# Seven-product feed-forward: each product of a set in its own PSUM tile, six tiles in rotation; the last spill begun from GpSimd's queue

## The chip, the core and the metric

The kernel runs on one core of a Trainium2 chip. The time is the device time of one execution of the whole program in microseconds, the median of several runs. TensorE multiplies matrices into PSUM, VectorE and ScalarE read PSUM and SBUF, GpSimd works on SBUF alone, and SyncE (SP) begins most of the DMAs. Each engine executes its own instructions strictly in their order and waits on semaphores for the others.

## The reference

A decoder trunk of two layers on 1024 tokens of width 1024, in float32. Each layer is a mixer (a pooling and state-space mixer in layer 0, two kinds of attention in layer 1) and a feed-forward, each followed by a layer norm. The change lies in the feed-forward, which is the same code for both layers:

```python
def swiglu(x, w_gate, w_up, w_down):
    return (jax.nn.silu(x @ w_gate) * (x @ w_up)) @ w_down

# in each layer
x = layer_norm(DEEPNORM_ALPHA * x + swiglu(x, w_gate[l], w_up[l], w_down[l]), g[l], b[l])
```

with `w_gate` and `w_up` of 1024 x 2816 and `w_down` of 2816 x 1024.

## The kernel before

**Seven products.** `ffn` computes each matrix product as a 2 x 2 block product with seven products of half-size blocks instead of eight (the Winograd form of Strassen's scheme): sums of blocks are formed first, seven products follow, and further sums put the result together. Each float32 operand is kept as a high part and a low part (`operand`: ScalarE's cast writes the high part, L195, VectorE's subtraction the low part, L203), and one product of operands takes three matmuls, high by high, high by low, low by high (L496 to L498).

**First half.** 2816 features are 22 tiles of 128, taken in 11 pairs. For each pair there is an even set (gate) and an odd set (up): 22 sets of seven products each. A product is 4 blocks of k by 3 matmuls of 128 x 128 by 128 x 512, 12 matmuls in one PSUM bank. `load` brings the weights of a set, `prep` forms the block sums and the operands for the set ahead, `prod` issues the matmuls, and `step(s, i)` does product i of set s with the additions on VectorE that use it. From the fourth set on the order is 1, 6, 2, 7, 5, 4, 3. Line by line: L509 is ScalarE's copy of product 1 into `u`, L519 adds product 6, L523 product 2, L527 product 7, L530 and L531 product 5, L535 product 4, L538 product 3. ScalarE applies SiLU to the gate's results (L545); GpSimd multiplies them by the up results (L543). `spill` forms four sums on GpSimd (L555 to L558) and stores seven blocks to DRAM (`parts`) from SP's queue (L562). `residual` scales the residual rows on GpSimd (L620, L621) and stores them from GpSimd's queue.

**PSUM.** There are eight banks: four tiles of one bank, `p0` to `p3`, and the tile `pa` of two banks, which exists twice. Products 1 and 2 of a set share one single tile one after the other, product 6 has another, products 7 and 5 are the two halves of one `pa`, and products 4 and 3 the two halves of the other `pa`. A wait is kept for each tile: product 5 into the second half waits until VectorE has read product 7 out of the first half.

**Second half.** `second` multiplies by `w_down` in the same way: the blocks come back from `parts` (`load2`, into `hr`), `prep2` forms the operands, and for each of seven products 11 steps of 12 matmuls (L628 to L630) go into four banks, one after three matmuls; the first product uses p0 to p3. `prep2` of the first product also replaces a quarter of each weight tile by a difference (L614), at once.

**What sets the order.** The program is written in one order; a scheduler then places the instructions on each engine's queue by their dependences and free buffers. SBUF holds 50 slots of 128 x 1024 that all tiles of these stages share, so a load waits until a slot is free.

Of the kernel before, what the change touches and what calls it, by code (L numbers as in the profile page):

```python
# [15 lines left out]
ALU = mybir.AluOpType  # L16
# [3 lines left out]
P = 128  # L20
# [60 lines left out]
class Trunk:  # L81
# [364 lines left out]
    def ffn(self, l, ln, store, rows, parts, nxt=None):  # L446
# [6 lines left out]
        nc, ap = self.nc, self.ap  # L453
        lo, hi = slice(0, 512), slice(512, 1024)
        mm = nc.tensor.matmul
        tt = nc.vector.tensor_tensor
        pt = nc.gpsimd.tensor_tensor
        n_pairs = NFF // 2
# [31 lines left out]
        def prod(s, i, out, ks=range(4)):  # L490
            a, b = ops[s][i], x7[i]
            if ks[-1] == 3:
                del ops[s][i]
            for k in ks:
                ah, al = a[:, k * P:(k + 1) * P], a[:, 512 + k * P:512 + (k + 1) * P]
                mm(out=out, lhsT=ah, rhs=b[k][:, lo], start=k == 0, stop=False)  # L496
                mm(out=out, lhsT=ah, rhs=b[k][:, hi], start=False, stop=False)  # L497
                mm(out=out, lhsT=al, rhs=b[k][:, lo], start=False, stop=k == 3)  # L498

        hid = {}  # L500

        def step(s, i, ks=range(4)):

            up = s % 2
            if i == 1:
                x = self.ps("p2" if up else "p0", 1)
                open_[s] = {"x": x, "u": self.slot(name="u")}
                prod(s, 1, x)
                nc.scalar.copy(out=open_[s]["u"][:, lo], in_=x)  # L509
                return  # L510
            o = open_[s]
            u, x = o["u"], o["x"]
            if i == 6:
                if ks[0] == 0:
                    o["v"] = self.ps("p3" if up else "p1", 1)
                v = o["v"]
                prod(s, 6, v, ks)
                if ks[-1] == 3:
                    tt(out=u[:, hi], in0=u[:, lo], in1=v, op=ALU.add)  # L519
            elif i == 2:  # L520
                prod(s, 2, x)
                o["c"] = [self.slot(name="c" if up else "h") for _ in range(2)]
                tt(out=o["c"][0][:, lo], in0=u[:, lo], in1=x, op=ALU.add)  # L523
            elif i == 7:
                o["wz"] = self.pa()
                prod(s, 7, o["wz"][:, lo])
                tt(out=u[:, lo], in0=u[:, hi], in1=o["wz"][:, lo], op=ALU.add)  # L527
            elif i == 5:
                prod(s, 5, o["wz"][:, hi])
                tt(out=o["c"][1][:, hi], in0=u[:, lo], in1=o["wz"][:, hi], op=ALU.add)  # L530
                tt(out=u[:, hi], in0=u[:, hi], in1=o["wz"][:, hi], op=ALU.add)  # L531
            elif i == 4:
                o["wz"] = self.pa()
                prod(s, 4, o["wz"][:, lo])
                tt(out=o["c"][1][:, lo], in0=u[:, lo], in1=o["wz"][:, lo], op=ALU.add)  # L535
            else:
                prod(s, 3, o["wz"][:, hi])
                tt(out=o["c"][0][:, hi], in0=u[:, hi], in1=o["wz"][:, hi], op=ALU.add)  # L538
            if i in (4, 3):
                c = o["c"][i == 4]  # L540
                if up:
                    h = hid[s // 2][i == 4]
                    pt(out=h, in0=h, in1=c, op=ALU.mult)  # L543
                else:
                    nc.scalar.activation(out=c, in_=c, func=AF.Silu)  # L545
                    hid.setdefault(s // 2, [None, None])[i == 4] = c
            if i == 3:
                del open_[s]

        def spill(p):  # L550

            h0, h1 = hid.pop(p)
            a11, a12, a21, a22 = h0[:, lo], h1[:, lo], h0[:, hi], h1[:, hi]
            s12, s34 = self.slot(name="s"), self.slot(name="s")
            pt(out=s12[:, lo], in0=a21, in1=a22, op=ALU.add)  # L555
            pt(out=s12[:, hi], in0=s12[:, lo], in1=a11, op=ALU.subtract)
            pt(out=s34[:, lo], in0=a11, in1=a21, op=ALU.subtract)
            pt(out=s34[:, hi], in0=a12, in1=s12[:, hi], op=ALU.subtract)  # L558
            for i, src in ((1, a11), (2, a12), (4, a22), (5, s12[:, lo]), (6, s12[:, hi]), (7, s34[:, lo]),
                           (3, s34[:, hi])):  # L560
                at = ((i - 1) * n_pairs + p) * P
                nc.sync.dma_start(out=parts[at:at + P, :], in_=src)  # L562


        flat = [(i, p) for i in (1, 6, 5, 2, 3, 7, 4) for p in range(n_pairs)]
        hr, we, wo, ops2 = {}, {}, {}, {}
        loaded = [self.load_ahead - 1]

        def load2(n):
            if n >= len(flat):  # L570
                return
            i, p = flat[n]
            if p % 2 == 0:
                m = min(2, n_pairs - p)
                at = ((i - 1) * n_pairs + p) * P
                r = self.slot(name="hr")
                nc.sync.dma_start(out=r[:, 0:m * 512].rearrange("p (a c) -> p a c", c=512),
                                  in_=parts[at:at + m * P, :].rearrange("(a p) c -> p a c", p=P))
                hr[i, p] = r[:, lo]
                if m > 1:  # L580
                    hr[i, p + 1] = r[:, hi]
            for w, first, k in ((we, 1, 0), (wo, 6, 1)):
                if i == first:
                    w[p] = self.load_raw(ap["ffn_w_down"][l, (2 * p + k) * P:(2 * p + k + 1) * P, :])

        def prep2(n):
            if n >= len(flat):
                return
            i, p = flat[n]
            a = self.operand(hr.pop((i, p)), None, "h")  # L590
            e, o = we[p], wo.get(p)
            last = []
            if i == 1:
                b = e[:, lo]
                last.append((e[:, lo], e[:, hi], e[:, lo], ALU.subtract))
            elif i == 6:
                b = self.slot(name="t")[:, lo]
                tt(out=b, in0=o[:, hi], in1=e[:, lo], op=ALU.subtract)
            elif i == 5:
                b = e[:, lo]  # L600
            elif i == 2:
                b = o[:, lo]
            elif i == 3:
                b = o[:, hi]
                last.append((o[:, lo], o[:, lo], o[:, hi], ALU.subtract))
            elif i == 7:
                b = e[:, hi]
                tt(out=b, in0=o[:, hi], in1=b, op=ALU.subtract)
            else:
                b = o[:, lo]  # L610
                tt(out=b, in0=b, in1=e[:, lo], op=ALU.add)
            ops2[n] = a, self.operand(b, None, "w")
            for out, in0, in1, op in last:
                tt(out=out, in0=in0, in1=in1, op=op)  # L614

        accs = []
# [74 lines left out]
        def leads():  # L691
            for i in (1, 2):
                for s in range(2):
                    step(s, i)
                if i == 1:
                    yield
            load(2)
            for g in (1, 2, 2):
                next(preps[g])
            yield  # L700
            step(2, 1)
            for k in range(4):
                for s in range(2):
                    step(s, 6, range(k, k + 1))
                if k == 0:
                    yield
                    step(2, 2)
                if k < 3:
                    yield
# [6 lines left out]
        for s in range(n_sets):  # L716
# [22 lines left out]
            if s == n_sets - 2:  # L739
                for n in range(self.load_ahead):  # L740
                    load2(n)
        vs = [self.slot(name="v") for _ in range(2)]
        spill(n_pairs - 1)
        x7 = self.x7 = None
        main = second()
# [1136 lines left out]
```

## Time and profile before

| | |
|---|---|
| median of three runs | 2664.48 us (2663.90 to 2668.51) |
| profiled execution, its own time | 2659.8 us |
| span of its instructions | 2657.9 us |
| TensorE busy | 94% of the span |
| VectorE, ScalarE, GpSimd busy | 69%, 39%, 28% |
| mean granted TensorE clock | 0.983 |

Busy time is the share of the span in which an engine has an instruction under way. The time outside the span, 1.9 us, belongs to no engine. The two feed-forwards' first halves run from about 520 to 996 us and from about 1955 to 2429 us of the span; their second halves follow at once.

### The profile page before, as it was taken

To read this page: it belongs to the slowest core of one execution; us is meant where nothing else is said; L and a number is where in the kernel's file an instruction comes from. 1 tells how busy PE (TensorE), PEld (TensorE's weight loads), DVE (VectorE), ACT (ScalarE), POOL (GpSimd) and SP (SyncE) were. 2 spreads that over 40 slices of the span, in tenths; PEclk is the share of its full clock that TensorE was granted. 3 is DMA by queue.
4 is the path that set the end of the run, shared out by engine and by line. 5 is a ranking of instruction groups with operands and counts; after the bars stand their busy time and mean duration, and the time that the engine had idled before them with its cause. 6 is when DMAs were issued, how large, how long until landed. Compare 5 with 4: busy or idle time off the path is not lost.

```text
span 2657.9 us, 31492 instructions
## 1 busy us (share of the span) xinstructions
PE 2509.7 (94%) x11886; PEld 2012.1 (76%) x11886; DVE 1832.9 (69%) x2922; ACT 1038.4 (39%) x1742; POOL 731.1 (28%) x408
## 2 busy tenths in 40 slices
PE   8999999999899899999999999999989989898998
PEld 6788777777777777887787777777767777777887
DVE  4454555787676758976655566787787676766988
ACT  3333434442222233463344455664452222222443
POOL 2544531114342521212011122111014252433103
PEclk9999999999999999999999999999999999999999
DMA  4111114223333337322100011112323333324742
GB/s 164 48 32 40 40 41 154 80 91 116 110 123 107 127 119 295 125 95 90 66 25 32 24 40 38 34 60 69 111 79 132 103 133 104 131 81 184 266 147 75
DMA packets 93847, 261.46 MB, mean 98 GB/s; under 512 B 9696, under 2 KB 9952, under 8 KB 93696
## 3 DMA queue, kind: packets, MB, share of 16 engines
q1 hardware_dynamic: 86496, 234.23, 25.6%
q0 software_dynamic: 4448, 15.27, 1.7%
q10 hardware_dynamic: 2752, 9.96, 1.0%
q8 instruction: 93, 1.52, 0.2%
q14 instruction: 58, 0.48, 0.1%
HBM read 185.89 MB, written 71.30 MB: 97 GB/s over the span
## 4 chain that ended last, share of the span: by engine, by line
PE 75%; DVE 13%; issue 5%; ACT 3%; POOL 2%; DMA 1%; SPq 0%; DVEq 0%; ACTq 0%; POOLq 0%
PE pa L496 5%; PE pa L498 5%; PE pa L497 5%; PE pa L236 5%; PE pa L238 4%; PE pa L237 4%; PE pa L1589 4%; DVE w L203 4%; PE p L236 3%; PE p L238 3%; PE p L237 3%; PE p L498 3%; PE p L496 3%; PE p L497 3%; PE p L1659 3%
## 5 line engine op out<-in xcount | busy, mean ns | idle before, releaser
L203 DVE TENSOR_TENSOR w<-wr,w 128x512 fp32r<-128x512 f32 x440 | 387.4, 897 | 80.4 <-ACT w L195 79.8
L195 ACT CAST w<-wr 128x512 fp32r<-128x512 f32 x440 | 252.8, 619 | 454.9 <-DVE wr L479 279.5
L496 PE MATMUL pa<-x,w 128*128 128x512 f32 x704 | 283.7, 406 | 64.1 <-DVE u L527 63.8
L543 POOL TENSOR_TENSOR h<-h,c 128x1024 f32<-128x1024 f32 x44 | 113.9, 2588 | 651.7 <-issue 449.3
L497 PE MATMUL pa<-x,w 128*128 128x512 f32 x704 | 282.5, 401 | 0.0
L498 PE MATMUL pa<-x,w 128*128 128x512 f32 x704 | 282.1, 401 | 0.0
L203 POOL TENSOR_TENSOR wl<-wr,wh 128x1024 fp32r<-128x1024 f32 (+2 forms) x55 | 130.6, 2377 | 447.9 <-ACT wh L195 414.6
L496 PEld LDWEIGHTS pa<-x,w 128*128 128x128 f32 x704 | 136.1, 193 | 109.6 <-DVE u L527 77.2
L496 PE MATMUL p<-x,w 128*128 128x512 f32 x528 | 207.3, 394 | 6.9 <-ACT w L195 6.9
L498 PE MATMUL p<-x,w 128*128 128x512 f32 x528 | 206.9, 392 | 0.1
L497 PE MATMUL p<-x,w 128*128 128x512 f32 x528 | 206.7, 392 | 0.1
L498 PEld LDWEIGHTS pa<-x,w 128*128 128x128 f32 x704 | 136.5, 194 | 30.2
L497 PEld LDWEIGHTS pa<-x,w 128*128 128x128 f32 x704 | 137.2, 195 | 27.9 <-DVE x L203 0.7
L236 PE MATMUL pa<-xh,wh 128*128 128x512 f32 x368 | 149.1, 405 | 1.9 <-ACT u L895 1.1
L238 PE MATMUL pa<-xh,wl 128*128 128x512 f32 x368 | 144.5, 393 | 4.3 <-POOL wl L203 4.3
L629 PE MATMUL p<-w,h 128*128 128x512 f32 x352 | 139.3, 396 | 7.2 <-DVE w L203 7.1
L237 PE MATMUL pa<-xl,wh 128*128 128x512 f32 x368 | 144.2, 392 | 0.0
L628 PE MATMUL p<-w,h 128*128 128x512 f32 x352 | 138.1, 393 | 5.8 <-ACT w L195 5.8
L630 PE MATMUL p<-w,h 128*128 128x512 f32 x352 | 138.2, 392 | 0.0
L203 DVE TENSOR_TENSOR h<-hr,h 128x512 fp32r<-128x512 f32 x154 | 124.2, 807 | 16.9 <-ACT h L195 16.8
L195 ACT CAST h<-hr 128x512 fp32r<-128x512 f32 x154 | 95.2, 618 | 91.2 <-DMA hr<-parts 65.7
L496 PEld LDWEIGHTS p<-x,w 128*128 128x128 f32 x528 | 99.7, 189 | 28.7 <-ACT w L195 8.0
(391 smaller groups left out, 6084.2 us busy)
## 6 DMA issues: line engine op xcount, KB each, us to landing
hr<-parts SPq DMA_DIRECT2D x70, 512.0 KB, 4.6
wr<-in_ffn_w_gate_dram SPq DMA_DIRECT2D x44, 512.0 KB, 4.2
wr<-in_ffn_w_up_dram SPq DMA_DIRECT2D x44, 512.0 KB, 4.3
parts<-s SPq DMA_DIRECT2D x88, 256.0 KB, 2.1
wr<-in_ffn_w_down_dram SPq DMA_DIRECT2D x44, 512.0 KB, 9.7
parts<-h SPq DMA_DIRECT2D x66, 256.0 KB, 2.1
accr<-rows SPq DMA_DIRECT2D x32, 512.0 KB, 3.6
wr<-in_even_wt_dram SPq DMA_DIRECT2D x24, 512.0 KB, 3.6
```

Source lines behind the costliest of these rows:

```text
L195: self.nc.scalar.copy(out=out, in_=in_)
L203: eng.tensor_tensor(out=out, in0=in_, in1=hi.bitcast(F32), op=ALU.subtract)
L236: mm(out=out, lhsT=lh, rhs=rh, start=i == 0, stop=False)
L237: mm(out=out, lhsT=lh, rhs=rl, start=False, stop=False)
L238: mm(out=out, lhsT=ll, rhs=rh, start=False, stop=i == n - 1)
L496: mm(out=out, lhsT=ah, rhs=b[k][:, lo], start=k == 0, stop=False)
L497: mm(out=out, lhsT=ah, rhs=b[k][:, hi], start=False, stop=False)
L498: mm(out=out, lhsT=al, rhs=b[k][:, lo], start=False, stop=k == 3)
L543: pt(out=h, in0=h, in1=c, op=ALU.mult)
L628: mm(out=out, lhsT=ah, rhs=b[:, lo], start=first, stop=False)
L629: mm(out=out, lhsT=ah, rhs=b[:, hi], start=False, stop=False)
L630: mm(out=out, lhsT=al, rhs=b[:, lo], start=False, stop=last)
```

## The change

- Each product has a tile of its own. `bank()` gives the tiles p0, p1, p2, p3, pa, pa in turn (of a `pa` only the first half is used), from product 7 of the first set on; products 1, 2 and 6 of the first three sets, which begin while the layer norm is still at work, keep their old tiles.
- The spill of the last pair is begun from GpSimd's queue; the others stay in SP's.
- In the first product of the second half the differences of L614 (L619 in the new text) are kept back: up to four wait in a list, and the oldest is issued behind the operands of a later step.

```diff
@@ -498,44 +499,45 @@
                 mm(out=out, lhsT=al, rhs=b[k][:, lo], start=False, stop=k == 3)
 
         hid = {}
+        turn = itertools.cycle(("p0", "p1", "p2", "p3", "pa", "pa"))
+
+        def bank():
+            tag = next(turn)
+            return self.pa()[:, lo] if tag == "pa" else self.ps(tag, 1)
 
         def step(s, i, ks=range(4)):
 
             up = s % 2
             if i == 1:
-                x = self.ps("p2" if up else "p0", 1)
+                x = self.ps("p2" if up else "p0", 1) if s < 3 else bank()
                 open_[s] = {"x": x, "u": self.slot(name="u")}
                 prod(s, 1, x)
                 nc.scalar.copy(out=open_[s]["u"][:, lo], in_=x)
                 return
             o = open_[s]
-            u, x = o["u"], o["x"]
+            u = o["u"]
             if i == 6:
                 if ks[0] == 0:
-                    o["v"] = self.ps("p3" if up else "p1", 1)
+                    o["v"] = self.ps("p3" if up else "p1", 1) if s < 2 else bank()
                 v = o["v"]
                 prod(s, 6, v, ks)
                 if ks[-1] == 3:
                     tt(out=u[:, hi], in0=u[:, lo], in1=v, op=ALU.add)
-            elif i == 2:
-                prod(s, 2, x)
+            else:
+                x = o["x"] if i == 2 and s < 3 else bank()
+                prod(s, i, x)
+            if i == 2:
                 o["c"] = [self.slot(name="c" if up else "h") for _ in range(2)]
                 tt(out=o["c"][0][:, lo], in0=u[:, lo], in1=x, op=ALU.add)
             elif i == 7:
-                o["wz"] = self.pa()
-                prod(s, 7, o["wz"][:, lo])
-                tt(out=u[:, lo], in0=u[:, hi], in1=o["wz"][:, lo], op=ALU.add)
+                tt(out=u[:, lo], in0=u[:, hi], in1=x, op=ALU.add)
             elif i == 5:
-                prod(s, 5, o["wz"][:, hi])
-                tt(out=o["c"][1][:, hi], in0=u[:, lo], in1=o["wz"][:, hi], op=ALU.add)
-                tt(out=u[:, hi], in0=u[:, hi], in1=o["wz"][:, hi], op=ALU.add)
+                tt(out=o["c"][1][:, hi], in0=u[:, lo], in1=x, op=ALU.add)
+                tt(out=u[:, hi], in0=u[:, hi], in1=x, op=ALU.add)
             elif i == 4:
-                o["wz"] = self.pa()
-                prod(s, 4, o["wz"][:, lo])
-                tt(out=o["c"][1][:, lo], in0=u[:, lo], in1=o["wz"][:, lo], op=ALU.add)
-            else:
-                prod(s, 3, o["wz"][:, hi])
-                tt(out=o["c"][0][:, hi], in0=u[:, hi], in1=o["wz"][:, hi], op=ALU.add)
+                tt(out=o["c"][1][:, lo], in0=u[:, lo], in1=x, op=ALU.add)
+            elif i == 3:
+                tt(out=o["c"][0][:, hi], in0=u[:, hi], in1=x, op=ALU.add)
             if i in (4, 3):
                 c = o["c"][i == 4]
                 if up:
@@ -559,12 +561,13 @@
             for i, src in ((1, a11), (2, a12), (4, a22), (5, s12[:, lo]), (6, s12[:, hi]), (7, s34[:, lo]),
                            (3, s34[:, hi])):
                 at = ((i - 1) * n_pairs + p) * P
-                nc.sync.dma_start(out=parts[at:at + P, :], in_=src)
+                (nc.gpsimd if p == n_pairs - 1 else nc.sync).dma_start(out=parts[at:at + P, :], in_=src)
 
 
         flat = [(i, p) for i in (1, 6, 5, 2, 3, 7, 4) for p in range(n_pairs)]
         hr, we, wo, ops2 = {}, {}, {}, {}
         loaded = [self.load_ahead - 1]
+        sums = []
 
         def load2(n):
             if n >= len(flat):
@@ -610,7 +613,9 @@
                 b = o[:, lo]
                 tt(out=b, in0=b, in1=e[:, lo], op=ALU.add)
             ops2[n] = a, self.operand(b, None, "w")
-            for out, in0, in1, op in last:
+            sums.extend(last)
+            while len(sums) > (4 if i == 1 else 0):
+                out, in0, in1, op = sums.pop(0)
                 tt(out=out, in0=in0, in1=in1, op=op)
 
         accs = []
```

**TensorE's queue, set 3, products 7 and 5.** The names `pa_656_4308` and `pa_659_4342` are tiles of PSUM; before, product 7 ends in the first, then come five matmuls of product 4 into the second, and product 5 goes into the first again:

```order
L497 MATMUL pa_656_4308<-x_611_3946,w_640_4215 128x512
L498 MATMUL pa_656_4308<-x_611_3946,w_640_4215 128x512
L496 MATMUL pa_659_4342<-x_575_3782,w_637_4191 128x512
L497 MATMUL pa_659_4342<-x_575_3782,w_637_4191 128x512
L498 MATMUL pa_659_4342<-x_575_3782,w_637_4191 128x512
L496 MATMUL pa_659_4342<-x_593_3863,w_637_4191 128x512
L497 MATMUL pa_659_4342<-x_593_3863,w_637_4191 128x512
L496 MATMUL pa_656_4308<-x_574_3778,w_641_4232 128x512
L497 MATMUL pa_656_4308<-x_574_3778,w_641_4232 128x512
```

After the change, at the same place:

```order
L497 MATMUL pa_663_4315<-x_611_3946,w_645_4220 128x512
L498 MATMUL pa_663_4315<-x_611_3946,w_645_4220 128x512
L499 MATMUL pa_663_4315<-x_611_3946,w_645_4220 128x512
L497 MATMUL pa_665_4332<-x_574_3778,w_647_4238 128x512
L498 MATMUL pa_665_4332<-x_574_3778,w_647_4238 128x512
L499 MATMUL pa_665_4332<-x_574_3778,w_647_4238 128x512
```

Product 5 follows product 7 directly, into another tile, and no part of product 4 is drawn ahead.

**VectorE's queue, start of an even set.** L203 makes low parts of weights (`w`), L519, L523 and L527 add products 6, 2 and 7, L477 to L486 form sums of weight blocks (`wr`). Before:

```order
L203 TENSOR_TENSOR w_943_6614<-wr_925_6469,w_943_6614 128x512
L203 TENSOR_TENSOR w_945_6631<-wr_925_6469,w_945_6631 128x512
L519 TENSOR_TENSOR u_942_6600<-u_942_6600,p1_944_6617 128x512
L523 TENSOR_TENSOR h_948_6659<-u_942_6600,p0_941_6599 128x512
L203 TENSOR_TENSOR w_950_6662<-wr_926_6471,w_950_6662 128x512
L477 TENSOR_TENSOR wr_926_6471<-wr_926_6471 128x512
L478 TENSOR_TENSOR wr_926_6471<-wr_925_6469,wr_926_6471 128x512
L527 TENSOR_TENSOR u_942_6600<-u_942_6600,pa_952_6671 128x512
L479 TENSOR_TENSOR wr_925_6469<-wr_926_6471,wr_925_6469 128x512
L486 TENSOR_TENSOR wr_925_6469<-wr_925_6469 128x512
L203 TENSOR_TENSOR w_951_6668<-wr_925_6469,w_951_6668 128x512
L203 TENSOR_TENSOR w_953_6685<-wr_926_6471,w_953_6685 128x512
```

After (the same lines are L204, L525, L531, L533 and L478 to L487 in the new text):

```order
L204 TENSOR_TENSOR w_880_5828<-wr_856_5671,w_880_5828 128x512
L204 TENSOR_TENSOR w_882_5845<-wr_856_5671,w_882_5845 128x512
L525 TENSOR_TENSOR u_879_5814<-u_879_5814,p1_881_5831 128x512
L531 TENSOR_TENSOR h_886_5874<-u_879_5814,p2_885_5861 128x512
L204 TENSOR_TENSOR w_888_5877<-wr_857_5673,w_888_5877 128x512
L478 TENSOR_TENSOR wr_857_5673<-wr_857_5673 128x512
L479 TENSOR_TENSOR wr_857_5673<-wr_856_5671,wr_857_5673 128x512
L533 TENSOR_TENSOR u_879_5814<-u_879_5814,p3_890_5886 128x512
L480 TENSOR_TENSOR wr_856_5671<-wr_857_5673,wr_856_5671 128x512
L487 TENSOR_TENSOR wr_856_5671<-wr_856_5671 128x512
L204 TENSOR_TENSOR w_889_5883<-wr_856_5671,w_889_5883 128x512
L204 TENSOR_TENSOR w_891_5900<-wr_857_5673,w_891_5900 128x512
```

Nothing moved here: the additions and the preparation of weights for the next set alternate as before, and only the tiles that the additions read are others.

**SP's queue behind the last set.** `hr` and `wr` are the loads for the second half, `parts` the spill of the last pair. Before:

```order
L577 DMA hr_963_6750<-parts_83 128x2x512
L224 DMA wr_964_6752<-in_ffn_w_down_dram 128x1024
L224 DMA wr_965_6754<-in_ffn_w_down_dram 128x1024
L562 DMA parts_83<-h_949_6660 128x512 x2
L562 DMA parts_83<-h_948_6659 128x512
L562 DMA parts_83<-s_981_6880 128x512 x2
L562 DMA parts_83<-s_982_6881 128x512 x2
L577 DMA hr_983_6893<-parts_83 128x2x512
L224 DMA wr_984_6895<-in_ffn_w_down_dram 128x1024
```

After:

```order
L580 DMA hr_1023_6810<-parts_83 128x2x512
L225 DMA wr_1024_6812<-in_ffn_w_down_dram 128x1024
L225 DMA wr_1025_6814<-in_ffn_w_down_dram 128x1024
L580 DMA hr_1046_6953<-parts_83 128x2x512
L225 DMA wr_1047_6955<-in_ffn_w_down_dram 128x1024
L225 DMA wr_1054_6979<-in_ffn_w_down_dram 128x1024
L580 DMA hr_1057_7000<-parts_83 128x2x512
```

The seven stores are gone from between the loads. On GpSimd's queue they now stand among the arithmetic of the last spill (`h` the products of gate and up, `s` the sums):

```order
L545 TENSOR_TENSOR h_1007_6718<-h_1007_6718,c_1031_6859 128x1024
L564 DMA parts_83<-h_1007_6718 128x512 x2
L545 TENSOR_TENSOR h_1006_6717<-h_1006_6717,c_1030_6858 128x1024
L557 TENSOR_TENSOR s_1044_6940<-h_1006_6717,h_1007_6718 128x512
L559 TENSOR_TENSOR s_1045_6941<-h_1006_6717 128x512
L558 TENSOR_TENSOR s_1044_6940<-s_1044_6940,h_1006_6717 128x512
L564 DMA parts_83<-h_1006_6717 128x512
L560 TENSOR_TENSOR s_1045_6941<-h_1007_6718,s_1044_6940 128x512
L564 DMA parts_83<-s_1044_6940 128x512 x2
L564 DMA parts_83<-s_1045_6941 128x512 x2
```

The first two stores come before the second multiplication, the others behind the sums that they store.

## Rows read from the trace of the kernel before

**Rows 1.** Page, part 1: busy us (share) xinstructions of each engine, whole span.

```profile
PE 2509.7 (94%) x11886; PEld 2012.1 (76%) x11886; DVE 1832.9 (69%) x2922; ACT 1038.4 (39%) x1742; POOL 731.1 (28%) x408
```

**Rows 2.** Windows: us; PE, PEld, DVE, ACT, POOL busy (x); PEclk; DMA; GB/s.

```profile
558.40:995.64 437.24, 406.86 (x1729) 329.68 (x1729) 298.58 (x371) 115.87 (x192) 161.09 (x87) 0.98 0.35 119
...
1992.45:2429.21 436.76, 406.39 (x1729) 329.35 (x1729) 298.70 (x371) 115.87 (x192) 161.12 (x87) 0.98 0.35 119
...
711.21:754.99 43.78, 40.23 (x168) 32.51 (x168) 29.78 (x37) 10.77 (x18) 17.07 (x10) 0.96 0.34 115
...
995.64:1020.46 24.82, 18.16 (x74) 13.38 (x72) 20.07 (x22) 1.92 (x4) 11.24 (x6) 0.98 0.46 159
...
2429.21:2453.45 24.24, 17.94 (x74) 13.28 (x72) 20.07 (x22) 1.76 (x3) 11.24 (x6) 1.00 0.44 158
...
1035.00:1100.00 65.00, 65.00 (x286) 53.14 (x285) 62.70 (x92) 32.82 (x60) 12.34 (x8) 1.00 0.63 225
```

**Rows 3.** Waits of PE, whole span: total us, times, longest us.

```profile
PE pa L496 <- DVE u L527: 63.8, 22, 3.7
```

**Rows 4.** PE timeline, one even set: start us, us, instruction, [idle before].

```profile
699.85 0.39 PE L496 MATMUL p<-x,w 128*128 128x512 f32 x1
...
708.01 0.39 PE L496 MATMUL pa<-x,w 128*128 128x512 f32 x1
...
711.94 0.50 PE L496 MATMUL pa<-x,w 128*128 128x512 f32 x1 [3.54 <-DVE u L527]
...
712.98 0.63 PE L496 MATMUL pa<-x,w 128*128 128x512 f32 x1
...
715.54 0.55 PE L496 MATMUL pa<-x,w 128*128 128x512 f32 x1
```

**Rows 5.** DVE timeline of the same stretch and the set behind it.

```profile
711.21 0.68 DVE L527 TENSOR_TENSOR u<-u,pa 128x512 f32<-128x512 f32 x1
...
744.28 5.64 DVE L203 TENSOR_TENSOR w<-wr,w 128x512 fp32r<-128x512 f32 x2 [2.04 <-ACT w L195]
...
754.99 0.67 DVE L527 TENSOR_TENSOR u<-u,pa 128x512 f32<-128x512 f32 x1
...
757.43 1.29 DVE L203 TENSOR_TENSOR w<-wr,w 128x512 fp32r<-128x512 f32 x2
```

**Rows 6.** POOL timeline: the run of work beside it.

```profile
738.58 2.64 POOL L543 TENSOR_TENSOR h<-h,c 128x1024 f32<-128x1024 f32 x1 [26.16 <-issue]
...
754.60 1.60 POOL L558 TENSOR_TENSOR s<-h,s 128x512 f32<-128x512 f32 x1
```

**Rows 7.** SP timeline: loads of the weights for the next even set.

```profile
735.85 2.14 SPq L224 DMA_DIRECT2D wr<-in_ffn_w_gate_dram  x2
```

**Rows 8.** PE timeline at the first set.

```profile
558.40 0.50 PE L496 MATMUL pa<-x,w 128*128 128x512 f32 x1 [1.66 <-DVE u L527]
```

**Rows 9.** SP timeline behind the last set: spill, then the loads queued behind.

```profile
996.37 9.74 SPq L562 DMA_DIRECT2D parts<-h  x3
...
1007.49 5.39 SPq L562 DMA_DIRECT2D parts<-s  x4
...
1012.98 0.39 SPq L577 DMA_DIRECT2D hr<-parts  x1
```

**Rows 10.** DVE timeline behind the last set, GpSimd at work from 1001.84.

```profile
1001.63 0.68 DVE L614 TENSOR_TENSOR wr<-wr 128x512 f32<-128x512 f32 x1
...
1002.23 0.68 DVE L203 TENSOR_TENSOR h<-hr,h 128x512 fp32r<-128x512 f32 x1
...
1003.54 2.77 DVE L614 TENSOR_TENSOR wr<-wr 128x512 f32<-128x512 f32 x1
...
1006.24 1.78 DVE L203 TENSOR_TENSOR h<-hr,h 128x512 fp32r<-128x512 f32 x1
```

**Rows 11.** DMA issues: KB each, median us from issue to landing.

```profile
rows<-accr POOLq DMA_DIRECT2D x16, 512.0 KB, 2.9
...
rows<-acc SPq DMA_DIRECT2D x16, 512.0 KB, 2.6
```

More of the change, by code (lines that the diff above doesn't have):

```diff
@@ L1 @@
+import itertools
 import math
```

## The prediction

> **What bounds the kernel now.** I read the page first. TensorE is busy for 94% of the span and no other engine for more than 69% [rows 1], so time can only come out of TensorE's idle time and out of time in which it runs slowly. The waits of TensorE come next: one line stands far above the others, product 5 waiting for L527, VectorE's addition of product 7, 22 times and 63.8 us in all [rows 3]; no other wait in that list reaches 7.2 us.
>
> The timelines show why. Up to 708.01 matmuls begin every 0.2267 us: from 699.85 to 708.01 there are 36 steps. Then TensorE stands for 3.54 us until product 5 begins at 711.94, directly behind the end of L527, which VectorE only began at 711.21 [rows 4, 5]. Product 5 does not need the sum u that L527 writes; it needs the tile, because products 7 and 5 are the two halves of one tile of `pa`. VectorE is late there because GpSimd works without a pause from 738.58 to 756.2 in this pattern (the even set before has the same run), and VectorE's own SBUF operations beside it stretch: two that take 1.29 us alone take 5.64 us [rows 5, 6].
>
> The wait costs more than itself. Behind it matmuls begin every 0.427 us (712.98 to 715.54, 6 steps), the 1.2 GHz level; then the 0.2267 us step of the 2.4 GHz level is back [rows 4]. The whole price is seen in the stage: a pair of sets is 168 matmuls, 38.1 us at 0.2267, and takes 43.78 us [rows 2].
>
> **The change part by part.** My sum starts from the profiled execution, 2659.8 us; the median of the three runs, 2664.48, lies 4.7 us above it, and I add that at the end.
>
> 1. *Own tiles for the products.* From the end of the first wait to the end of the last set, one feed-forward takes 437.24 us and the other 436.76 us for 1728 matmul steps each [rows 2]; 1728 x 0.2267 = 391.7. The excess is 45.5 + 45.1 = **90.6 us**, waits and slow matmuls together. In the new order product 5 goes to another tile than product 7 and follows it directly; nothing of L527 is left before it. I take all 90.6 as removed, if nothing else is late in its place. What is next:
>
>    - *The banks.* A bank comes back six products later, 6 x 2.72 = 16.3 us after its last owner began. L527's counterpart, the latest addition today, ends 17.1 us after GpSimd's run began (738.58 to 755.66) [rows 5, 6]. GpSimd's run starts some 1.3 us behind the end of the up set's product 4, and product 7 of the next set ends five products (13.6 us) after that. So the bank is read at about 18.4 on a clock that starts with the end of product 4, and wanted at 10.9 + 16.3 = 27.2. Slack 8.8 us: no wait.
>    - *The weights.* VectorE's order around it stays as it is (the second pair of fences). The pieces 6 and 7 of the following set are done at 757.43 + 1.29 = 758.72, 20.1 us after GpSimd's run began, which is 21.4 on that clock; piece 6 is wanted nine products after product 4's end, 24.5. Slack **3.1 us**. This is the thinnest place, and today's stall hides it.
>    - *VectorE's load.* 29.78 us of work in a pair [rows 2] against 38.1: 78%.
>
> 2. *The first set.* Today's 1.66 us wait [rows 8] lies outside those windows. Product 5 now takes the bank of the first set's product 6, whose addition is the second instruction ahead of L527 in VectorE's queue, so about 1.2 us (two steps of 0.60 [rows 10]) earlier: 0.5 us stay. Gain 1.2 x 2 = **2.4 us**. The first three sets prepare weights with less lead; bound there: nothing, or a wait as long as today's 1.66 in each feed-forward. I take 1.5 x 2 = **3 us lost**.
>
> 3. *Into the second half.* Behind the last set 74 matmuls (16.8 us) take 24.82 and 24.24 us [rows 2]: an excess of 15.4 us, in part the wait for loads that SP's queue holds behind the last spill until 1012.98 [rows 9]. With the spill in GpSimd's queue those loads are issued when their slots come free. Against that: the second half takes all of p0 to p3 at once, and the last two products now lie in p0 and p1. GpSimd's multiply on product 4's result, 2.4 to 2.6 us, starts about 1.4 us before the last product ends; one VectorE operation waits it out, one more follows, then the addition of the last product, 0.6 each, done about 2.7 us behind that product's end. Five matmuls (1.1 us) cover it, so 1.6 us of waiting. The three deferred differences then stand ahead of the fourth step's operands. The first meets GpSimd's second multiply (2.77 us today), the others the spill's arithmetic (1.78) [rows 10]: those operands come at 2.7 + 2.8 + 4 x 1.8 = 12.7 us, where TensorE wants them at 1.6 + 3 x 2.72 = 9.8, 2.9 us of waiting. Together 4.5 us instead of today's 7.7: a gain of 3.2 x 2, **6 us**. Bounds: a gain of all 15.4, or a loss of 9 if the loads are no earlier and the new waits come on top. Less **2** because VectorE is busy for 62.7 of 65 us right behind it [rows 2] and has little to catch up with.
>
> 4. *GpSimd's queue.* Seven issues are added twice, 0.3 us dearer to landing than SP's by the only pair of alike stores, 2.9 against 2.6 us [rows 11]. Nothing on GpSimd waits behind them until the second product's additions, some 30 us later. The read-back that needs them is that of the last pair, ten steps (27 us) into the second half; the spill is issued by 12 us. Cost nothing. In the other sets only SP's spill order and the residual's store move by one place: nothing.
>
>    A rule speaks against this part. The Trainium skill, "SBUF — State Buffer", section "SBUF: two separate sides", says that descriptors of a DMA issued by GpSimd are built by that engine and stall while VectorE holds the shared port; its figures are about 620 ns alone and 3100 ns beside VectorE, so seven issues would be some 17 us late (an estimate from that page) and the last pair's read-back about 5 us: the sum would be 10 us higher. Rows 11 do not show it for stores beside the same VectorE work, so I keep my value.
>
> Sum: 2659.8 - 90.6 - 2.4 + 3 - 6 + 2 = 2565.8 for a profiled execution, + 4.7 = 2570.5, forecast **2570 us**, 3.5% faster.
>
> **The rivals.**
>
> *VectorE becomes the bound.* For it: the 3.1 us of slack, and the next even set's weights, whose two loads are begun from 735.85 to 738.0 [rows 7] and whose first use is the 5.64 us row at 744.28 [rows 5]; a faster TensorE asks for them sooner. Against it: 78% load. Price: if none of its 37 operations a pair (0.60 each, 22.2 us) overlapped GpSimd's 17.07 us [rows 2], a pair would take 39.3 us, 1.2 over the floor; over 18 pairs 22 us: 2592. If operands came so late that half of the excess returned: 2570 + 45 = 2615.
>
> *The change doesn't do what it says.* If product 5 had really waited for something that L527 merely precedes, the stall would stay: about 2664. Against it: L527 is the named releaser in all 22, and product 5 begins within 0.1 us of its end.
>
> *Slower: the clock.* Six banks in rotation could cost TensorE its higher level at each change of bank. A matmul at 1.2 GHz costs 0.2 us more [rows 4]; the gain of 94 us is gone when 470 of the 3456 matmuls (14%) run so, about one and a half in each product. With three of twelve, 864 x 0.2 = 173 us: 2570 + 173 = 2743. Against it: the second half changes its bank after every three matmuls and shows a granted clock of 1.00 there [rows 2]. The Trainium skill, "TensorE: Matmul & The Clock Gate", section "A second HAM failure mode: psum-queue depth-cycling", tells of a kernel whose cycling through PSUM banks made the clock swing between its levels; by that rule this rival would win. The trace does not bear it out.
>
> **How the numbers follow.** Forecast, with its own range 2555 to 2588: 0.77. VectorE as the bound, 2590 to 2617: 0.15. No effect, 2664: 0.04. Slower by the clock: 0.04. The low end is everything gone: 2659.8 - 90.6 - 3.3 - 15.4 + 4.7 = 2555, and 2554 as the end. About 0.7 lies in the forecast's own range; to reach 0.8 the upper end goes into the first rival, to 2606. The bound for same is 0.2%, 5 us, about what a measurement of this kernel can tell: faster 0.92, same 0.04, slower 0.04.
>
> **What would show it.** In the changed profile the wait of product 5 on the addition of product 7 should be gone from TensorE's list; pairs of sets should take 38 to 38.6 us at a granted clock of 1.00; VectorE's busy time in a pair should stay at 30 us; SP should issue the loads of the second half before GpSimd's last spill is done. The step on weights is wrong if TensorE's list shows a wait for `w` (L204 or L196) inside the sets; the step on banks if it shows one for an addition into `u`, `c` or `h`; the step on the second half if the first 74 matmuls there take over 24 us. The forecast falls if pairs take over 40 us.

## The result, and the profile after

The changed kernel takes 2558.17 us (2553.97 to 2562.32) where the kernel before takes 2665.69 (2663.9 to 2668.51): a ratio of 0.960 with the interval 0.957 to 0.962, 4.0% faster. In a second set of runs beside the kernel before it took 2558.86 us, ratio 0.961 (0.959 to 0.962). 2570 was forecast, in a range from 2554 to 2606. The profiled execution took 2555.2 us with a span of 2553.4, 104.5 us under the span before; the forecast had 94.0 on that scale.

Page, part 1, and then the waits of TensorE over the whole span (total us, times, longest us):

```profile
PE 2475.8 (97%) x11886; PEld 2000.4 (78%) x11886; DVE 1835.8 (72%) x2922; ACT 1037.1 (41%) x1742; POOL 719.3 (28%) x422
```

```profile
PE p L497 <- ACT w L196: 4.8, 2, 2.4
...
PE p L633 <- DVE c L540: 3.6, 2, 1.8
```

The 63.8 us behind the addition of product 7 [rows 3] are gone; that line (now L533) does not stand in the list at all. New is L633, the second half's start, waiting for the last product's addition L540, once in each feed-forward. Apart from it only two additions of the sets are waited for, both at the start of each feed-forward: L531 for 0.5 us and L525 for 0.2 us.

Where the 104.5 us came from is seen when both spans are cut at the same instructions: first half, second half, the layers between, first half, last stretch. Windows (us; PE, PEld, DVE, ACT, POOL busy (x); PEclk; DMA; GB/s) of the kernel before, then of after:

```profile
515.62:995.64 480.02, 444.33 (x1894) 358.29 (x1892) 334.62 (x441) 140.53 (x234) 161.09 (x87) 0.98 0.33 115
995.64:1171.74 176.10, 169.44 (x734) 137.81 (x732) 150.90 (x248) 75.63 (x131) 34.23 (x20) 0.99 0.53 187
1171.74:1950.05 778.31, 740.91 (x3968) 589.00 (x3966) 537.97 (x1017) 391.87 (x760) 125.36 (x76) 0.98 0.17 55
1950.05:2429.20 479.15, 443.59 (x1893) 357.88 (x1892) 334.72 (x441) 140.53 (x234) 161.11 (x87) 0.98 0.33 115
2429.20:2657.90 228.70, 213.86 (x925) 173.69 (x923) 202.14 (x330) 90.31 (x161) 55.49 (x26) 0.99 0.48 168
```

```profile
516.30:948.74 432.44, 428.85 (x1894) 351.57 (x1892) 338.07 (x445) 144.27 (x242) 151.00 (x87) 1.00 0.38 135
948.74:1118.44 169.70, 167.88 (x734) 138.48 (x733) 149.03 (x244) 70.87 (x123) 37.13 (x27) 0.99 0.50 175
1118.44:1898.59 780.15, 740.55 (x3968) 588.71 (x3966) 537.68 (x1017) 392.25 (x760) 127.73 (x76) 0.98 0.17 55
1898.59:2330.92 432.33, 428.80 (x1893) 351.48 (x1892) 337.97 (x445) 144.29 (x242) 151.59 (x87) 1.00 0.39 134
2330.92:2553.40 222.48, 211.58 (x925) 174.35 (x923) 200.49 (x326) 85.92 (x153) 58.02 (x33) 0.98 0.45 159
```

The first halves give 47.6 + 46.8 = 94.4 us, the second halves some 13.4 (6.4 in the first feed-forward, 7.0 in the last up to its last matmul); the layers between and the ends, which the change does not touch, take 3.3 us more. These untouched layers differ from run to run: from the last matmul of one feed-forward to the first of the next, TensorE's timelines show 730.8 to 743.6 us over all kernels of this study. So the effects below that are smaller than some 10 us are read from their own stage.

The windows that answer to [rows 2]: the sets behind the first wait (557.34 and 1939.56 are where product 5 of the first set begins), the 74 matmuls at the start of each second half, and one pair.

```profile
557.34:948.74 391.40, 391.40 (x1727) 324.23 (x1727) 303.28 (x377) 119.21 (x200) 151.00 (x87) 1.00 0.40 142
1939.56:2330.92 391.36, 391.36 (x1726) 324.19 (x1727) 303.21 (x377) 119.22 (x200) 151.59 (x87) 1.00 0.41 142
...
948.74:969.06 20.32, 18.50 (x75) 14.76 (x73) 20.18 (x20) 0.62 (x1) 14.02 (x13) 0.92 0.43 145
2330.92:2351.26 20.34, 18.52 (x74) 14.78 (x73) 20.20 (x20) 1.24 (x2) 14.03 (x13) 0.92 0.42 148
621.80:659.82 38.02, 38.02 (x170) 31.49 (x169) 29.93 (x38) 10.55 (x18) 15.90 (x9) 1.00 0.39 132
```

The sets run without a gap: busy time equals the window, the granted clock is 1.00, a pair takes 38.02 us where it took 43.78. VectorE's work in it is what it was, 29.93 us.

### The profile page after: what moved, and what is told of

Read it like the earlier page. It is cut to its first block, busy times and chain, and to the rows that moved or that the text cites. A ratio compares the mean times of both kernels' runs of the same rounds, so it can differ in the third digit from the quotient of the medians.

```text
span 2553.4 us, 31570 instructions
## 1 busy us (share of the span) xinstructions
PE 2475.8 (97%) x11886; PEld 2000.4 (78%) x11886; DVE 1835.8 (72%) x2922; ACT 1037.1 (41%) x1742; POOL 719.3 (28%) x422
## 4 chain that ended last, share of the span: by engine, by line
PE 85%; DVE 7%; issue 3%; ACT 3%; POOL 1%; DMA 1%; SPq 0%; DVEq 0%; ACTq 0%; POOLq 0%
PE p L497 7%; PE p L498 7%; PE p L499 7%; PE pa L237 5%; PE pa L239 4%; PE pa L238 4%; PE pa L1594 4%; PE pa L499 3%; PE pa L497 3%; PE p L237 3%; PE pa L498 3%; PE p L239 3%; PE p L238 3%; PE p L633 3%; PE p L635 3%; PE p L634 3%
## 5 line engine op out<-in xcount | busy, mean ns | idle before, releaser
L204 DVE TENSOR_TENSOR w<-wr,w 128x512 fp32r<-128x512 f32 x440 | 415.9, 968 | 105.0 <-ACT w L196 99.2
L497 PE MATMUL p<-x,w 128*128 128x512 f32 x848 | 331.3, 392 | 6.4 <-ACT w L196 4.8
L498 PE MATMUL p<-x,w 128*128 128x512 f32 x848 | 331.2, 391 | 0.5 <-DVE x L204 0.4
L499 PE MATMUL p<-x,w 128*128 128x512 f32 x848 | 330.8, 390 | 0.1
L204 POOL TENSOR_TENSOR wl<-wr,wh 128x1024 fp32r<-128x1024 f32 (+2 forms) x55 | 133.0, 2421 | 447.0 <-ACT wh L196 415.8
L497 PEld LDWEIGHTS p<-x,w 128*128 128x128 f32 x848 | 159.2, 188 | 43.4 <-ACT w L196 6.4
L498 PEld LDWEIGHTS p<-x,w 128*128 128x128 f32 x848 | 159.3, 188 | 35.7 <-DVE x L204 3.5
L499 PEld LDWEIGHTS p<-x,w 128*128 128x128 f32 x848 | 159.2, 188 | 33.8 <-DVE w L204 1.0
L497 PE MATMUL pa<-x,w 128*128 128x512 f32 x384 | 149.5, 389 | 0.0
L498 PE MATMUL pa<-x,w 128*128 128x512 f32 x384 | 149.5, 389 | 0.0
L499 PE MATMUL pa<-x,w 128*128 128x512 f32 x384 | 149.5, 389 | 0.0
L633 PE MATMUL p<-w,h 128*128 128x512 f32 x352 | 138.4, 394 | 3.6 <-DVE c L540 3.6
L204 DVE TENSOR_TENSOR h<-hr,h 128x512 fp32r<-128x512 f32 x154 | 123.5, 802 | 10.7 <-ACT h L196 10.6
L635 PE MATMUL pa<-w,h 128*128 128x512 f32 x264 | 102.9, 390 | 0.0
```

Of the source, the lines that this page charges most:

```text
L204: eng.tensor_tensor(out=out, in0=in_, in1=hi.bitcast(F32), op=ALU.subtract)
L633: mm(out=out, lhsT=ah, rhs=b[:, lo], start=first, stop=False)
L635: mm(out=out, lhsT=al, rhs=b[:, lo], start=False, stop=last)
```

## The experiments

**1. Why product 5 waited: the tile, or VectorE's order and SP's queue.** The kernel before with the two small edits alone (the list of differences, and GpSimd's queue for the last spill):

> The two small edits without the tiles: products 7 and 5 share a tile as before. Theory (product 5 waits because of the tile): the wait on L527 stays, 22 times and about 63 us in all, pairs take 43.8 us, and only the start of the second half gets better: 2651 us (2647 to 2656). Rival (the sets stalled for another reason, SP's queue or VectorE's order, which the small edits touch): the waits shrink and the time falls below 2640 us.

Measured: 2656.56 us, ratio 0.996 (0.995 to 0.998), 0.6 us past the upper end of what was expected. TensorE's waits:

```profile
PE pa L496 <- DVE u L527: 64.0, 22, 3.8
```

The wait is untouched, and the first halves take 479.0 and 481.8 us. The small edits do not reach it. To the last matmul the second halves are 3.4 and 4.1 us shorter than before, 7.5 in all.

**2. The tiles alone.**

```diff
-                (nc.gpsimd if p == n_pairs - 1 else nc.sync).dma_start(out=parts[at:at + P, :], in_=src)
+                nc.sync.dma_start(out=parts[at:at + P, :], in_=src)
...
-            while len(sums) > (4 if i == 1 else 0):
+            while sums:
```

> The change without its two small edits: each product in its own tile, but the last spill in SP's queue and the differences at once. Theory: the tiles carry the first halves (94.4 us of the 104.5 us by which the spans differ), the two small edits carry the start of the second half (13.4 us there): about 2570 us (2566 to 2574), and the first 74 matmuls of the second half take 24 us or more, as in the kernel before (24.82, 24.24), not 20.3. Rival: the start of the second half is better because the sets in front of it no longer stall, so the tiles carry it too: 2558 to 2562 us, 74 matmuls in 20 to 21 us.

Measured: 2560.27 us, ratio 0.960 (0.957 to 0.963), inside the rival's bounds. The first halves take 432.8 and 432.3 us, as in the changed kernel. The 74 matmuls take 22.2 and 21.0 us, between the theory's 24 and the rival's 20.3. To the last matmul the second halves are 7.4 us shorter than before and 6.0 us longer than after: the theory gave all 13.4 us there to the small edits, but the tiles bring 7.4 by themselves and the small edits 7.5 (experiment 1), about half each. SP's queue behind the last set, which ends at 948.11 here, shows what the tiles do there:

```profile
949.44 6.13 SPq L564 DMA_DIRECT2D parts<-h  x3
956.95 5.40 SPq L564 DMA_DIRECT2D parts<-s  x4
962.44 0.39 SPq L580 DMA_DIRECT2D hr<-parts  x1
```

The loads are still held behind the spill, but it ends 14.3 us behind the last set, not 17.3 (995.64 to 1012.98 [rows 9]): GpSimd's second multiplication, which the later stores wait for, begins 4.4 us behind the last set and not 6.2 (1001.84 [rows 10]).

**3. The two small edits one by one.** The changed kernel with the first, then with the second of the two lines of experiment 2:

> The changed kernel with the last spill back in SP's queue. Theory: the loads of the second half are again held behind the spill, and this part is worth most of the 13.4 us gained there: 2567 us (2563 to 2571), with a wait of TensorE on operands made from late loads. Rival: the loads had slack, and the queue is worth nothing: 2557 to 2560 us, 74 matmuls in 20.3 us.

> The changed kernel with each difference issued at once. Theory: two of them now stand ahead of the last product's addition in VectorE's queue, 0.6 us each where they meet nothing; the wait for bank p1 grows from 1.8 to about 3.0 us in each feed-forward: 2561 us (2559 to 2564). Rival: they move work that is late anyway, and nothing changes: 2557 to 2559 us.

Measured: 2560.43 us (ratio 0.960, 0.957 to 0.962) and 2561.43 us (0.959, 0.956 to 0.962), neither told from the changed kernel's 2558.17. By the stage, the spill in SP's queue makes the second halves 1.6 + 1.5 = 3.1 us longer; the differences at once leave them as they are (to within 0.1 us). The waits of the second half with the spill in SP's queue, first feed-forward:

```profile
PE p L633 <- DVE c L540: 1.8, 1, 1.8
PE p L634 <- DVE w L204: 1.1, 3, 0.5
```

So both expectations put too much on one edit. What GpSimd's queue changes stands in SP's queue of the changed kernel:

```profile
934.65 0.38 SPq L580 DMA_DIRECT2D hr<-parts  x1
...
938.73 2.37 SPq L225 DMA_DIRECT2D wr<-in_ffn_w_down_dram  x2
962.03 0.33 SPq L580 DMA_DIRECT2D hr<-parts  x1
```

Two loads `hr` and four `wr` go from 14.1 to 8.0 us before the second half begins; the next goes 13.3 us into it, when a store of the last spill has landed. With the spill in SP's queue all of them wait, until 13.1 us into the second half, and these late loads cost some 1.5 us in a feed-forward.

Beside a spill in GpSimd's queue the list of differences is worth nothing: the wait for bank p1, 1.9 us without it and 1.8 with it, is not what sets the end of this stretch (experiment 6). Beside a spill in SP's queue it is worth 2.9 us, the 6.0 of experiment 2 less the 3.1 here; there the first load behind the spill goes 13.1 us into the second half with the list and 14.3 without.

**4. Why VectorE was late.**

> The kernel before, products 7 and 5 still in one tile, without the four sums that GpSimd forms for each pair but the last; the stores read the products in their place, so that the output is not the reference's. GpSimd's run in a pair falls from 17 to some 10.4 us. Theory (VectorE is late because GpSimd works beside it): operations that take 1.7 us beside those sums take 0.6 us again, VectorE is some 4 us earlier at L527, and the 3.5 us waits go without any new tile: about 2575 us (2560 to 2595), pairs near 38.1 us. Rival (VectorE is late because weights reach ScalarE late: the row at 744.28 stood 2.04 us for it): the 22 waits stay near 3.5 us and the time near 2660 us.

The edit to the kernel before, for all pairs but the last:

```diff
-            pt(out=s12[:, lo], in0=a21, in1=a22, op=ALU.add)
...
-            pt(out=s34[:, hi], in0=a12, in1=s12[:, hi], op=ALU.subtract)
+            s12, s34 = h1, h0
```

Measured in a single run: 2597.37 us, just past the theory's range and far from the rival's 2660. TensorE's waits for L527, one steady pair, and the VectorE row that the rival rests on:

```profile
PE pa L496 <- DVE u L527: 10.4, 6, 1.9
```

```profile
722.48:761.04 38.56, 38.56 (x169) 31.39 (x168) 24.95 (x37) 10.66 (x18) 10.57 (x5) 1.00 0.37 130
```

```profile
734.67 2.33 DVE L203 TENSOR_TENSOR w<-wr,w 128x512 fp32r<-128x512 f32 x1 [2.04 <-ACT w L195]
```

The tile is still shared, GpSimd's run is 10.57 us, and the pair takes 38.56 us without a wait. The row that stood 2.04 us for ScalarE still does, and nobody waits for what comes of it: the rival falls. L527 begins 12.9 us behind the start of GpSimd's run (728.90 to 741.79), where it was 16.4 [rows 5, 6]. The edit also ends the pair's spill earlier, and SP issues the loads behind it 14.5 us after that start and not 18.1; what this does by itself was not tried. The six waits left lie early in the two first halves (the last at 665.36 and 2070.36); with the slow matmuls behind them and the old second half they keep the time above the theory's range. So both were needed for the stall: a shared tile, and VectorE late beside GpSimd. With either one away, steady pairs show no stall.

**5. How much the banks have to spare.** Two kernels that differ in the line of `turn` only:

```diff
-        turn = itertools.cycle(("p0", "p1", "p2", "p3", "pa", "pa"))
+        turn = itertools.cycle(("pa", "pa"))
...
+        turn = itertools.cycle(("pa", "pa", "p3"))
```

> The changed kernel with a turn of two tiles (pa, pa) in place of six. Theory (a bank is wanted some 10.9 us plus 2.72 us for each tile in the turn behind the end of the up set's product 4, and read 18.4 us behind it): with two it is wanted at 16.3 and read at 18.4, so each pair waits some 2.1 us for L533 and runs slowly for a while behind that: 22 waits, 2615 to 2655 us. Rival (it only matters that products 7 and 5 do not share a tile): no waits inside the sets, 2555 to 2562 us.

> The changed kernel with a turn of three tiles (pa, pa, p3). Theory: the bank is wanted at 10.9 + 8.2 = 19.1 us and read at 18.4: 0.7 us to spare, so no wait or one below 1 us in a pair, 2555 to 2570 us. If waits over 1 us show, the slack of 8.8 us that the prediction gave to six tiles is too large by what they show.

Measured in a single run each: 2627.55 us and 2595.82. The waits of two tiles, then of three:

```profile
PE pa L497 <- DVE u L525: 22.0, 16, 1.4
PE pa L497 <- DVE u L533: 20.0, 18, 1.9
PE pa L497 <- DVE u L536: 12.8, 16, 0.8
```

```profile
PE pa L497 <- DVE u L536: 8.9, 10, 0.9
...
PE p L497 <- DVE u L536: 5.4, 6, 0.9
```

```profile
629.18:668.71 39.53, 38.62 (x169) 31.38 (x169) 29.94 (x37) 10.55 (x18) 15.91 (x9) 1.00 0.37 127
```

With two tiles the time is in the expected range, but the waits are three a pair (1.37, 1.01 and 0.80 us) and not one; the rival, by which any two tiles would do, falls. With three the time is 25.8 us past the expected range: the waits come to 14.3 us in all, and the first halves take 13.3 and 13.7 us more than in the changed kernel. Product 7's addition L533 costs nothing, as worked out; late by 0.9 us is the second addition of product 5, L536, which the prediction had not looked at. Three more tiles of 2.72 us each less this 0.9 make 7.3 us to spare for six tiles (an estimate from these rows), not 8.8. The slack was real, and its bottleneck another instruction.

**6. What sets the start of the second half.** A turn begun two places earlier, and the same with the first three differences on GpSimd:

```diff
+        turn = itertools.cycle(("pa", "pa", "p0", "p1", "p2", "p3"))
...
+                (pt if i == 1 and n < 7 else tt)(out=out, in0=in0, in1=in1, op=op)
```

> The changed kernel with the turn begun two places earlier (pa, pa, p0, p1, p2, p3), so that the last two products of a first half lie in pa and not in p0 and p1, which the second half takes at once. Theory: the 1.8 us wait for p1 goes, but the operands of the fourth step, done 11.5 us into the second half behind the three differences, are then wanted at 3 x 2.72 = 8.2: a wait of about 3 us for w takes its place, and the first 74 matmuls take 20.5 to 22 us (20.3 in the changed kernel): nothing gained. Rival: the slow stretch behind the first wait was what the bank cost, and without it 74 matmuls take 17 to 18.5 us.

> The same turn, and the first three differences on GpSimd, between and behind the multiplications of the last pair, so that VectorE goes from the last addition straight to the fourth step's operands. Theory: both waits go, 74 matmuls take 17 to 18.5 us instead of 20.3, and two feed-forwards save 4 to 7 us: 2551 to 2555 us beside 2558. Rival: GpSimd works some 5 us longer beside VectorE and makes those operands as late as the differences did: 74 matmuls in 20 us or more, 2557 to 2563 us.

> The changed kernel itself once more, on the same chip as the two others: 2553 to 2563 us, 74 matmuls in 20.3 us.

Measured: 2565.67 us for the first (a single run), 2553.13 for the second (ratio 0.958, 0.957 to 0.959) and 2558.86 for the changed kernel. The 74 matmuls take 22.7 and 20.2 us, 20.4 and 20.2, 20.3 and 20.2. TensorE's first wait in the second half, with the shifted turn, which begins it at 948.20:

```profile
959.75 0.80 PE L634 MATMUL p<-w,h 128*128 128x512 f32 x1 [3.01 <-DVE w L204]
```

This is the theory, with the 74 matmuls 0.7 us over its bounds in one feed-forward (3.0 us of waiting, then slow matmuls) and 0.3 under them in the other: the wait for the bank goes, and a wait of 3.0 us for the fourth step's operands comes. The second halves are 2.2 us longer in all and the first halves 1.5 us shorter than in the changed kernel; the rest of its longer time lies in the untouched layers. Those operands are there 11.5 us into the second half whichever bank is taken. In the second run of the changed kernel TensorE waits for p1 and then for them, too (waits, first feed-forward):

```profile
PE p L633 <- DVE c L540: 1.8, 1, 1.8
PE p L634 <- DVE w L204: 0.9, 1, 0.9
```

In the first profile of the changed kernel the second wait does not show, because seven matmuls behind the first wait began 0.427 us apart and TensorE came to the fourth step later by itself; the 74 matmuls take 20.3 us both times. VectorE's chain there:

```profile
951.12 0.68 DVE L540 TENSOR_TENSOR c<-u,p 128x512 f32<-128x512 f32 x1
951.71 5.14 DVE L619 TENSOR_TENSOR wr<-wr 128x512 f32<-128x512 f32 x3
956.78 1.78 DVE L204 TENSOR_TENSOR h<-hr,h 128x512 fp32r<-128x512 f32 x1
958.48 1.78 DVE L204 TENSOR_TENSOR w<-wr,w 128x512 fp32r<-128x512 f32 x1
```

Three differences that take 1.8 us where they meet nothing take 5.14 beside GpSimd. Moved to GpSimd they only move the wait on to the fifth step (1.9 us), and the stage is no shorter; the 5.7 us between the medians are not explained by it, so that kernel's gain stays open.

**7. GpSimd off VectorE's back.** The shifted turn, and the four sums of the last spill on VectorE:

```diff
+            add2 = tt if p == n_pairs - 1 else pt
-            pt(out=s12[:, lo], in0=a21, in1=a22, op=ALU.add)
+            add2(out=s12[:, lo], in0=a21, in1=a22, op=ALU.add)
```

> The shifted turn, with the four sums of the last spill on VectorE, so that GpSimd is done after its second multiplication, 5.7 us into the second half. Theory (those operands are late because VectorE works beside GpSimd): behind the multiplication each operation takes 0.6 us, seven of them end at about 5.7 + 4.2 = 9.9 us, 1.7 us behind the 8.2 at which the fourth step is wanted; 74 matmuls take 18.3 to 19.3 us (20.2 with the shifted turn alone): 2552 to 2557 us. Rival: the four operations more that stand ahead of those operands on VectorE cost what they save, 74 matmuls in 20 us or more: 2557 to 2562 us.

Measured: 2552.10 us (2551.2 to 2555.5), ratio 0.955 (0.953 to 0.957). The 74 matmuls take 19.0 us in both feed-forwards, inside the theory's bounds. VectorE from 948.77, when the second half has run for 3.0 us:

```profile
948.77 3.48 DVE L620 TENSOR_TENSOR wr<-wr 128x512 f32<-128x512 f32 x2
952.17 0.68 DVE L558 TENSOR_TENSOR s<-h,h 128x512 f32<-128x512 f32 x1
...
955.18 0.68 DVE L204 TENSOR_TENSOR h<-hr,h 128x512 fp32r<-128x512 f32 x1
955.78 0.68 DVE L204 TENSOR_TENSOR w<-wr,w 128x512 fp32r<-128x512 f32 x1
```

With four operations more ahead of them the fourth step goes on 10.7 us into the second half, 0.8 us earlier than with the shifted turn alone, because behind GpSimd's multiplication each takes 0.6 us; TensorE still waits 2.2 us for it. This is the best version of the study: by the stages 1.3 us in each second half and 1.0 in each first half better than the changed kernel, some 4.5 us, of which the shifted turn alone gives 0.5 and 0.9 in the first halves. The intervals of the two ratios do not overlap, but they come from different sets of runs, and the kernel before took 2672.24 us in this one.

**8. All spills from GpSimd's queue.**

> The changed kernel with all spills begun from GpSimd's queue, not only the last. Theory: by the rows of the last spill (four issues in 2.15 us) seven issues put some 3.9 us into GpSimd's run of 17 us, nothing waits for it, and the time stays at 2555 to 2563 us. Rival: the issues lengthen GpSimd's work beside VectorE, and the weights, 3.1 us to spare, come late: waits on w inside the sets, over 2580 us. The Trainium skill, SBUF — State Buffer, section SBUF: two separate sides, gives about 3100 ns for an issue beside VectorE; by that figure seven would take 21.7 us (an estimate from that page), GpSimd would need more than a pair of sets takes, and the time would pass 2600 us.

Measured in a single run: 2566.3 us, past the expected 2563 by what the untouched layers take more here; the first halves take 433.6 and 432.7 us, and the sets behind the first show no wait. Issues of GpSimd, and two of VectorE's operations beside them:

```profile
624.00 2.15 POOL L564 DMA_DIRECT2D parts<-s  x4
...
650.22 0.58 POOL L564 DMA_DIRECT2D parts<-h  x1
```

```profile
648.19 7.94 DVE L204 TENSOR_TENSOR w<-wr,w 128x512 fp32r<-128x512 f32 x2 [2.22 <-ACT w L196]
```

The same two in the changed kernel:

```profile
648.15 4.97 DVE L204 TENSOR_TENSOR w<-wr,w 128x512 fp32r<-128x512 f32 x2 [3.17 <-ACT w L196]
```

An issue takes 0.54 to 0.58 us beside VectorE. VectorE's two operations take 7.94 us and not 4.97, so the first half of the rival is seen: VectorE's work comes later. No wait on `w` follows from it. The stores land after a median of 2.3 and 2.9 us against 2.1 from SP's queue.

## Why the prediction was right, step by step

1. *Own tiles.* 90.6 us forecast, and (437.24 - 391.40) + (436.76 - 391.36) = 91.2 measured. The mechanism is shown: experiments 1 and 2 separate the tile from everything else, and experiment 4 what made VectorE late. Of the three covers, the bank's was put at 8.8 us and is 7.3 by experiment 5, and it hangs on L536; the weights' 3.1 us were not measured, but no wait for `w` shows inside the sets, not even in experiment 8, where two of VectorE's operations take 3.0 us longer; VectorE's load is 29.93 of 38.02 us, 79%.
2. *The first sets.* 2.4 - 3 forecast, 94.4 - 91.2 = 3.2 us gained. The wait at product 5 of the first set fell to 0.17 us instead of 0.5, and the loss did not come: the wait for the first weights fell from 3.45 to 2.40 us instead of growing. Why it fell was not tried; with the shifted turn it is 3.5 us again and the first halves are no longer than here.
3. *Into the second half.* The term that was mis-sized: 6 - 2 = 4 us forecast, 13.4 measured, inside the bounds given. The new wait for p1 is there as worked out (1.8 us for 1.6), and so are the fourth step's operands (11.5 us for 12.7, a wait of 0.9 or the same time in slow matmuls for 2.9). Three steps failed. The late loads were credited to GpSimd's queue alone: six loads go ahead of the last spill by it, as the prediction had it, but with the tiles in place it gives only 3.1 of the 13.4 us (experiment 3), while the tiles, which shorten the spill's way, give 7.4 by themselves (experiment 2). The excess before did not end with the 74 matmuls: they give 8.4 of the 13.4, and the next 58, which took 14.5 and 15.2 us and take 13.1 now, 3.4 more. And the 2 us set against a busy VectorE were not lost: the rest of the second halves is 1.6 us shorter.
4. *GpSimd's queue.* Cost nothing, as forecast, even for all spills (experiment 8). The Trainium skill, "SBUF — State Buffer", section "SBUF: two separate sides", gives its 3100 ns for a DMA begun by GpSimd while VectorE runs a `tensor_copy`, which VectorE does not run in these sets. Beside the additions and subtractions that it runs, an issue takes 0.54 to 0.58 us in this trace, so the 10 us that the prediction worked out from that figure did not come.

The sum: 91.2 + 3.2 + 13.4 - 3.3 (untouched stretches) = 104.5 us.

The rivals: VectorE did not become the bound of the sets. The change does what it says: without the tiles the wait for L527 stays (experiment 1). The clock did not fall: with six banks in turn the sets run at a granted clock of 1.00. The Trainium skill, "TensorE: Matmul & The Clock Gate", section "A second HAM failure mode: psum-queue depth-cycling", has the swing come from short idle times between groups of matmuls; the sets of the changed kernel show none, so they show that a turn of six banks by itself does not bring it.

## What to carry to other kernels

A wait is kept for the tile, not for the half of it that is written: two results with different readers belong into different tiles, if banks are free. Ask first why the reader is late, since taking either cause away removes the stall. And where a wait is removed at the seam of two stages, work out when each later operand is ready: a bank freed earlier gains nothing while the operands' own chain ends later.

## What the runs showed of the hardware

A wait of TensorE costs more than itself, and not by a fixed sum. Against the 38.0 us of a pair without waits, one wait of 0.90 us costs 1.5 (three tiles), three of 3.2 us together cost 4.2 (658.66 to 700.84 with two tiles, 42.18 us), one of 3.54 costs 5.8 (43.78 us). The same wait of 1.8 us was followed by seven matmuls 0.427 us apart in one profile of the changed kernel and by none in the other.

VectorE's operations on two SBUF tiles take 0.6 us alone and some 1.7 beside GpSimd's sums (three of L619 take 5.14 us, experiment 6), while an addition that reads PSUM stays at 0.67 us beside them (L527 at 754.99 beside L558 at 754.60 [rows 5, 6]). The Trainium skill, "SBUF — State Buffer", section "SBUF: two separate sides", has the port shared by the two as a lock held for an instruction, against VectorE operations with two SBUF inputs; the rows agree. Four such operations were better moved onto the loaded VectorE than left on GpSimd (experiment 7).
